# A hybrid encoder on one core: TensorE's order of state-space units and attention steps written out, matrices prepared in three parts and three units ahead

## The chip, the core and the metric

One core of a Trainium2 chip runs the whole kernel. Its engines are TensorE (PE; its weight loads are listed as PEld), VectorE (DVE), ScalarE (ACT), GpSimd (POOL) and SyncE (SP). Each works through its own queue in order; semaphores tie the queues together. The metric is the device time of one execution in microseconds, from start to end.

## The reference

Two layers of an encoder over 512 positions of width 1024, float32. The first layer joins a state-space mixer and grouped-query attention; the second is a recurrent block. Each is followed by a feed-forward part. The change lies in the first layer's mixer alone, so only that is shown.

```python
# state-space mixer, per direction (0 forward, 1 backward)
bu_re = jnp.einsum("bsgc,gpc->bsgp", uf, bb_re)
bu_im = jnp.einsum("bsgc,gpc->bsgp", uf, bb_im)
_, _, h_re, h_im = lax.associative_scan(_complex_linear_combine,
    (abar_re, abar_im, bu_re, bu_im), reverse=(direction == 1), axis=1)
y = y + (jnp.einsum("bsgp,gcp->bsgc", h_re, c_re[direction])
         - jnp.einsum("bsgp,gcp->bsgc", h_im, c_im[direction]))
...
g = jax.nn.gelu(y)
out = g * jax.nn.sigmoid(g @ glu_w + glu_b)
# attention, per block of 128 queries
s = jnp.einsum("bqkgd,bskd->bkgqs", q_blk, kf)
p = jax.nn.softmax(s, axis=-1)
o = jnp.einsum("bkgqs,bskd->bqkgd", p, vf)
# both are joined
mix = jnp.concatenate([y_s5, y_att], axis=-1) @ hyb_w_out[e]
```

## The kernel before

The mixer runs as eight **units**, four groups of columns (`pg`) times two directions (`d`), while attention runs as 32 **steps**, one for a head and a block of 128 queries. Steps and units share the engines; they do not depend on each other. What is left of attention behind the eight units is done in the **fill**, together with the gate's and the output's first products.

A unit has these parts, by the names in the code:

- `s5_prep` builds its matrices: complex products on GpSimd (L341, L343, L345), copies on ScalarE (L356 into `s5c`, L364 into `s5bt`, L369 into `s5bx`), four transposes on TensorE (L363). `s5_lag` follows: sixteen small products on TensorE (L406) and four sums on VectorE into `s5dc` (L415 for d = 0, L421 for d = 1).
- `s5_phase` copies phase tables on ScalarE (L384 to L390).
- `s5_states` has two halves. Each is a product on TensorE (L441, into PSUM `pb` in the first half and `p` in the second), three operations on VectorE that turn it by the phase (L446, L447, L448) and two scans (L455).
- `s5_turn` turns the states back: four products on GpSimd (L466, L468, L467, L469 in the order of its queue), two sums on VectorE (L472 needs L466 and L468, L473 needs L467 and L469), and sixteen matmuls on TensorE (L477) that add the unit's output to `py`.
- After two units, `s5_out` adds the direct part (L488), copies (L490) and transposes (L493, L494); `s5_ut` brings the next group's input (L500, L502).

A step of attention has scores (L967, L968), their maximum on VectorE (L970, out `esum`), the exponential on ScalarE (L972), four transposes (L980) with a copy (L982), and for two steps together sixteen products with the values (L989). The transposes are those of an earlier step, so a step doesn't wait for its own exponential.

PSUM has two banks `p5` for all that the code calls `p` (the second half's states, L363, L406, L493, L500 and the small L686), one `pb`, one `py`, two for scores, one each for `po` and `pt`.

The loop calls units in turn, with `STEPS[i]` steps of attention in each, and calls `prep(i + 2)` in unit i; units 0 and 1 are prepared ahead of it. In units 3 and 4 it also closes a pair of adaptive vectors (L686, L691). The order of calls is not the order on the engines: a scheduler in the framework orders each engine's queue, TensorE's too, by its own estimate of when things are ready. Behind the loop, TensorE's order is the written one.

## Time and profile before

| what | value |
|---|---|
| median of 3 runs | 1255.64 us (1254.99 to 1257.53) |
| the profiled execution | 1256.23 us |
| its span, first to last instruction | 1254.4 us |
| mean granted clock of TensorE | 0.959 |
| busy: TensorE | 1161.8 us (93%) |
| busy: VectorE | 804.5 us (64%) |
| busy: ScalarE | 532.3 us (42%) |
| busy: GpSimd | 240.4 us (19%) |

Times inside the kernel are microseconds from the span's start. The loop of eight units and its steps lies between about 122 and 262 us, the fill between 265 and 305 us. Shares over the whole span say little on the loop, since its stretches have different limits: it is read from windows and from timelines of single engines. A granted clock of 1.00 is TensorE's upper level, 0.50 the lower. Rows that follow each other on VectorE overlap by about 0.08 us: an operation of 512 columns is listed with 0.68 us and the next one starts 0.60 later.

### The profile page before, as it was taken

What the parts mean: (1) busy time and instruction counts of PE and PEld (TensorE: products, weight loads), DVE (VectorE), ACT (ScalarE), POOL (GpSimd) and SP (SyncE); (2) the same over time, 40 slices, a digit from 0 to 9 for tenths busy, and PEclk for the clock granted to TensorE, in tenths of its full rate; (3) what the DMA queues carried; (4) which work ended last, traced back from release to release, by engine and by line L of the source; (5) the groups of instructions that cost most, each with busy time, mean ns of one, the idle gap of its engine ahead of it and who ended that gap; (6) DMA issues with size and microseconds to landing.
All of it is one profiled execution on the core that took longest, in us unless ns stands there. A gap on an engine that the chain in (4) does not pass through costs nothing.

```text
span 1254.4 us, 16894 instructions
## 1 busy us (share of the span) xinstructions
PE 1161.8 (93%) x6456; PEld 983.0 (78%) x6456; DVE 804.5 (64%) x1182; ACT 532.3 (42%) x962; POOL 240.4 (19%) x346
## 2 busy tenths in 40 slices
PE   3678798889999999999999999789999999999997
PEld 2568577667998888888888988569988888888887
DVE  7548897988789875678433789995753332445243
ACT  3147577645452332134322449853543321334130
POOL 9996995410000000000000053000000000000000
PEclk9989697979999999999999999789999999999998
DMA  9411301065538765667332332112242223322311
GB/s 337 130 56 58 113 20 35 2 201 153 194 108 272 265 205 190 208 204 248 102 101 85 101 109 76 51 56 79 73 129 88 98 101 101 90 96 101 101 34 67
DMA packets 83856, 151.74 MB, mean 121 GB/s; under 512 B 5696, under 2 KB 30272, under 8 KB 83776
## 3 DMA queue, kind: packets, MB, share of 16 engines
q1 hardware_dynamic: 75712, 137.04, 33.6%
q10 hardware_dynamic: 8064, 13.64, 3.5%
q8 instruction: 50, 0.82, 0.3%
q14 instruction: 30, 0.25, 0.1%
HBM read 148.55 MB, written 2.10 MB: 120 GB/s over the span
## 4 chain that ended last, share of the span: by engine, by line
PE 71%; DVE 13%; POOL 8%; ACT 3%; issue 2%; DMA 1%; SPq 0%; ACTq 0%; DVEq 0%; POOLq 0%
PE ps L560 13%; PE ps L561 12%; PE ps L559 12%; PE px L559 8%; PE px L561 8%; PE px L560 8%; DVE wl L513 2%; POOL tiny L76 1%; DVE actb L455 1%; DMA wr<-wout 1%; PE py L477 1%; PE po L989 1%; DVE ti L1411 1%; DVE hs L1410 1%; DVE esum L970 1%
## 5 line engine op out<-in xcount | busy, mean ns | idle before, releaser
L513 DVE TENSOR_TENSOR wl<-wr,wh 128x1024 fp32r<-128x1024 f32 (+2 forms) x175 | 211.3, 1208 | 298.4 <-ACT wh L512 291.5
L512 ACT CAST wh<-wr 128x1024 fp32r<-128x1024 f32 (+2 forms) x170 | 173.6, 1022 | 436.5 <-PE ps L560 200.1
L560 PE MATMUL ps<-actb,wh 128*128 128x512 f32 (+1 forms) x512 | 181.3, 354 | 0.1
L559 PE MATMUL ps<-acta,wh 128*128 128x512 f32 (+1 forms) x328 | 116.8, 357 | 0.0
L561 PE MATMUL ps<-acta,wl 128*128 128x512 f32 (+1 forms) x328 | 116.1, 355 | 0.0
L559 PE MATMUL ps<-hid,wh 128*128 128x512 f32 x288 | 112.1, 389 | 0.0
L561 PE MATMUL ps<-hid,wl 128*128 128x512 f32 x288 | 112.0, 389 | 0.0
L560 PE MATMUL ps<-hid,wh 128*128 128x512 f32 x288 | 112.0, 389 | 0.0
L560 PEld LDWEIGHTS ps<-actb,wh 128*128 128x128 f32 x512 | 97.7, 191 | 13.5 <-DVE actb L849 0.3
L559 PE MATMUL px<-hid,wh 128*128 128x512 f32 (+1 forms) x288 | 98.9, 343 | 0.0
L560 PE MATMUL px<-hid,wh 128*128 128x512 f32 (+1 forms) x288 | 98.5, 342 | 0.0
L561 PE MATMUL px<-hid,wl 128*128 128x512 f32 (+1 forms) x288 | 98.5, 342 | 0.0
L560 PE MATMUL px<-actb,wh 128*128 128x512 f32 (+1 forms) x224 | 85.5, 382 | 0.0
L641 DVE SCALAR_TENSOR_TENSOR acc<-wr,cact,acc 128x1024 f32<-128x1024 f32 x49 | 62.8, 1282 | 16.8 <-DMA wr<-ada_w 16.3
L559 PEld LDWEIGHTS ps<-acta,wh 128*128 128x128 f32 x328 | 63.0, 192 | 8.5
L561 PEld LDWEIGHTS ps<-acta,wl 128*128 128x128 f32 x328 | 62.7, 191 | 8.5
L1338 POOL MEMSET xp<- 128x2 f32 x8 | 0.7, 98 | 348.0 <-PE px L561 343.7
L559 PE MATMUL ps<-actc,wh 128*128 128x512 f32 (+1 forms) x184 | 65.1, 354 | 0.0
L561 PE MATMUL ps<-actc,wl 128*128 128x512 f32 (+1 forms) x184 | 64.8, 352 | 0.0
L559 PEld LDWEIGHTS ps<-hid,wh 128*128 128x128 f32 x288 | 54.1, 188 | 11.2
L560 PEld LDWEIGHTS ps<-hid,wh 128*128 128x128 f32 x288 | 54.1, 188 | 11.2
L561 PEld LDWEIGHTS ps<-hid,wl 128*128 128x128 f32 x288 | 54.0, 188 | 11.2
(504 smaller groups left out, 2709.8 us busy)
## 6 DMA issues: line engine op xcount, KB each, us to landing
wr<-w SPq DMA_DIRECT2D x128, 512.0 KB, 3.7
wr<-ada_w SPq DMA_DIRECT2D x56, 512.0 KB, 4.4
wr<-wout SPq DMA_DIRECT2D x16, 512.0 KB, 3.6
araw<-ada_w ACTq DMA_DIRECT2D x32, 256.0 KB, 3.1
wr<-win SPq DMA_DIRECT2D x16, 512.0 KB, 3.8
acta<-ada_w SPq DMA_DIRECT2D x16, 256.0 KB, 5.5
actb<-ada_w SPq DMA_DIRECT2D x16, 256.0 KB, 5.5
nt<-ada_w ACTq DMA_DIRECT2D x16, 256.0 KB, 2.9
```

Of the source, the lines that this page charges most:

```text
L76: self.eng.tensor_scalar(t, a, s, None, op0=op0)
L455: self.scan = V.tensor_tensor_scan(*z, 0.0, op0=ALU.mult, op1=ALU.add)
L477: mm(p4[:, x], h[:, o:o + P], c[:, x], start=(d == 0 and x == 0 and i == 0), stop=False, skip_group_check=True)
L512: nc.scalar.copy(hi, src)
L513: (lo_eng or nc.vector).tensor_tensor(lo, src, hi.bitcast(F32), op=ALU.subtract)
L559: mm(out, wh, xh, start=first and a == a0 and lead(o), stop=False, skip_group_check=True)
L560: mm(out, wh, xl, start=False, stop=False, skip_group_check=True)
L561: mm(out, wl, xh, start=False, stop=last and a == a0 + kk - 1, skip_group_check=True)
L641: nc.vector.scalar_tensor_tensor(acc, raw, self.ca[:, k:k + 1], acc, op0=ALU.mult, op1=ALU.add)
L970: nc.vector.reduce_max(nb, s, axis=AX.X, negate=True)
L989: self.nc.tensor.matmul(po[h2 * 64:h2 * 64 + 64, t * 128:(t + 1) * 128], self.vp[:, kb, p // 2], pts[h2][:, kb * 128:(kb + 1) * 128], star ...
L1410: V.tensor_tensor_scan(hs, a[:, 0], ti[:, 0], 0.0, op0=ALU.mult, op1=ALU.add)
```

## The change

`s5_prep` becomes a generator of three parts (products and copies; transposes; the lag), `s5_states` yields after each half, `s5_out` has two parts, and `s5_turn` hands back a function that issues L477 later. The loop is written out as `unit(i)`: the whole of it stands in `manual()`, in which TensorE keeps the order of the code. The other engines' queues are still ordered by the scheduler. Unit 2 is prepared ahead of the loop and unit i+3 in unit i, one unit earlier than before. Of the attention steps, 25 are taken in the loop (2 in unit 0, 3 in each of the seven others, 2 behind them), where it was 23. The number of instructions of each engine is otherwise the same, and the program behind the loop is the same apart from the two steps. Lines of the new kernel are 4 to 10 higher (L441 is L445, L472 and L473 are L475 and L476, L477 is L483, L970 is L980, L686 is L696).

```diff
-STEPS = ((2, 2),) * 5 + ((2, 1),) + ((0, 0),) * 2
+STEPS = ((0, 0, 2),) + ((1, 1, 1),) * 7
+LAST = 2
...
+        sl0 = 3 if d == 0 else 0
+        bx = []
+        for j, src in enumerate((vr, vi)):
+            t = self.tl(tp, f"s5bx{j}", [P, 4, 4, 16], bufs=1)
+            A.copy(t, src[:, :, sl0].unsqueeze(2).to_broadcast([P, 4, 4, 16]))
+            bx.append(t)
+        yield
...
         self.s5u[(pg, d)] = bt, cs
-        return bx, cs
+        yield
+        self.s5_lag(tp, pg, (bx, cs), d)
+        yield
...
                 self.scan = V.tensor_tensor_scan(*z, 0.0, op0=ALU.mult, op1=ALU.add)
-        return vr, vi
...
+            yield vr, vi
...
+        def outputs(py):
+            p4 = py.rearrange("p (x g n) -> p x g n", x=4, g=2)
+            for i, (h, c) in enumerate(((a, cr), (vr, ci))):
+                for x in range(4):
+                    o = (x % 2 * 2 + x // 2) * P
+                    mm(p4[:, x], h[:, o:o + P], c[:, x], start=(d == 0 and x == 0 and i == 0), stop=False, skip_group_check=True)
+
+        return outputs
...
-        for i in range(8):
...
+        def steps(n):
+            for _ in range(n):
+                self.step(att)
+
+        def outputs(i):
+            if i % 2 == 0:
+                pys.append(self.psum("py"))
+            turns[i](pys[i // 2])
+
+        def unit(i):
             pg, d = i // 2, i % 2
+            pr = prep(i + 3) if i < 5 else iter(())
+            next(pr, None)
             if d == 0:
                 gts.append(self.tl(self.hp, "h", [P, 512], bufs=9))
             e = self.s5_phase(lp, pg, d, self.POST[i][0])
             if i == 3:
                 self.s5_tables(sp, 1)
+            st = self.s5_states(lp, pg, d, *e, uts[pg])
+            next(st)
+            steps(STEPS[i][0])
+            v = next(st)
+            next(st, None)
+            turns.append(self.s5_turn(pg, d, e[0], *v, self.POST[i][1]))
+            steps(STEPS[i][1])
+            so = iter(())
+            if i:
+                outputs(i - 1)
+                if d == 0:
+                    so = out(pg - 1)
+                    next(so)
+            next(pr, None)
+            if d == 0 and pg < 3:
+                uts.append(self.s5_ut(lp, sz[pg + 1]))
+            steps(STEPS[i][2])
+            next(so, None)
+            next(pr, None)
+            if i == 4:
+                next(pr, None)
+                pctx.close()
+                self.weights(rctx, 3, 2, side="right")
             if i in FIN:
...
+        turns = []
+        with self.manual():
+            for _ in prep(2):
+                pass
+            uts.append(self.s5_ut(lp, sz[0]))
+            for i in range(8):
+                unit(i)
+            steps(LAST)
+            outputs(7)
+            for _ in out(3):
+                pass
```

What this moves is seen at three places. In the names, `pb_` and `p_` are the states of a unit's two halves, `pa_` scores, `actb` states and their turned sums; the numbers tell buffers apart.

TensorE, around the end of unit 3 (its second half is `p_446` before and `p_447` now; `pb_486` and `pb_490` are unit 4's first half). Before:

```order
L477 MATMUL py_1833<-s5c_109,actb_1799 128x128 x4
L441 MATMUL pb_486_2233<-s5ut_2021,s5bt_1911 64x128 x8
L980 MATMUL pt_1967<-consts_sb,pexp_1855 128x128 x4
L686 MATMUL p_472_2177<-ones,h_810 128x1 x4
L956 MATMUL pt_1974<-consts_sb,qr_1129 128x128
```

Now:

```order
L1049 MATMUL pt_2126<-consts_sb,tmp_2124 128x128 x4
L990 MATMUL pt_2139<-consts_sb,pexp_2039 128x128 x4
L410 MATMUL p_471_2146<-s5c_104,s5bx_433_1993 64x128 x2
L410 MATMUL p_471_2146<-s5c_105,s5bx_434_1995 64x128 x2
L410 MATMUL p_471_2146<-s5c_104,s5bx_433_1993 64x128 x2
L410 MATMUL p_471_2146<-s5c_105,s5bx_434_1995 64x128 x2
L696 MATMUL p_473_2161<-ones,h_810 128x1 x4
L445 MATMUL pb_490_2213<-s5ut_1925,s5bt_1744 64x128 x8
```

The small L686 (L696 now) stood behind unit 4's first state product and two other products; now it stands between the lag of unit 6 and that state product. It takes the PSUM bank of unit 3's second half in both.

TensorE, where unit 1's output is added. Before, from its first half on (`pb_444` is unit 3's):

```order
L477 MATMUL py_1457<-s5c_104,actb_1653 128x128 x4
L967 MATMUL pa_376_1767<-kth_1102,q_305_1487 128x512
L968 MATMUL pa_376_1767<-ktl_1103,q_305_1487 128x512
L406 MATMUL p_413_1922<-s5c_116,s5bx_411_1918 64x128 x2
L406 MATMUL p_413_1922<-s5c_117,s5bx_412_1920 64x128 x2
L406 MATMUL p_413_1922<-s5c_116,s5bx_411_1918 64x128 x2
L406 MATMUL p_413_1922<-s5c_117,s5bx_412_1920 64x128 x2
L980 MATMUL pt_1773<-consts_sb,pexp_1687 128x128 x4
L989 MATMUL po_1566<-pts_1765,vp 64x128
L441 MATMUL pb_444_2046<-s5ut_1607,s5bt_1730 64x128 x8
L477 MATMUL py_1457<-s5c_105,actb_1619 128x128 x4
```

Now (`p_405` is unit 2's second half):

```order
L445 MATMUL p_405_1860<-s5ut_1562,s5bt_1437 64x128 x8
L977 MATMUL pa_409_1884<-kth_1102,q_332_1569 128x512
L978 MATMUL pa_409_1884<-ktl_1103,q_332_1569 128x512
L990 MATMUL pt_1890<-consts_sb,pexp_1755 128x128 x4
L483 MATMUL py_1735<-s5c_104,actb_1698 128x128 x4
L483 MATMUL py_1735<-s5c_105,actb_1643 128x128 x4
L496 MATMUL py_1735<-s5cd_1383,s5ut_1464 128x2x64 x4
L371 MATMUL p_415_1914<-consts_sb,s5vr_1781 128x128 x2
L371 MATMUL p_415_1914<-consts_sb,s5vi_1782 128x128 x2
L510 MATMUL p_416_1920<-consts_sb,h_814 128x128 x4
```

The two halves of L477 stood apart, with unit 3's first state product between them; now they stand together (L483) behind unit 2's second state product.

VectorE, from unit 4's first half (before) and from unit 4's end (now), up to unit 5's first half (`pb_544` before, `pb_522` now). Before:

```order
L455 SCALAR_TENSOR_TENSOR actb_2229<-s5m4t_2220,pb_486_2233 128x255
L455 SCALAR_TENSOR_TENSOR actb_2230<-s5m4t_2220,pb_486_2233 128x255
L472 TENSOR_TENSOR actb_2076<-actb_2076,actb_2077 128x511
L446 TENSOR_TENSOR s5m_2257<-s5e_2219,p_488_2248 128x512
L447 TENSOR_TENSOR p_488_2248<-s5e_2219,p_488_2248 128x512
L448 TENSOR_TENSOR p_488_2248<-p_488_2248,s5m_2257 128x512
L473 TENSOR_TENSOR actb_2042<-actb_2042,actb_2043 128x511
L455 SCALAR_TENSOR_TENSOR actb_2229<-s5m4t_2220,p_488_2248 128x255
L455 SCALAR_TENSOR_TENSOR actb_2230<-s5m4t_2220,p_488_2248 128x255
L446 TENSOR_TENSOR s5m_2482<-s5e_2459,pb_544_2473 128x512
```

Now:

```order
L459 SCALAR_TENSOR_TENSOR actb_2209<-s5m4t_2200,p_498_2256 128x255
L459 SCALAR_TENSOR_TENSOR actb_2210<-s5m4t_2200,p_498_2256 128x255
L980 TENSOR_REDUCE esum_1198<-pa_511_2323 128x1
L475 TENSOR_TENSOR actb_2271<-actb_2271,actb_2272 128x511
L476 TENSOR_TENSOR actb_2209<-actb_2209,actb_2210 128x511
L425 SCALAR_TENSOR_TENSOR s5dc_120<-p_516_2350,consts_sb,s5dc_120 128x4x16
L425 SCALAR_TENSOR_TENSOR s5dc_120<-p_516_2350,consts_sb,s5dc_120 128x4x32
L701 TENSOR_TENSOR mod_2166<-p_517_2367,cols_sb 128x4
L425 SCALAR_TENSOR_TENSOR s5dc_120<-p_516_2350,consts_sb,s5dc_120 128x4x48
L425 SCALAR_TENSOR_TENSOR s5dc_120<-p_516_2350,consts_sb,s5dc_120 128x256
L450 TENSOR_TENSOR s5m_2396<-s5e_2373,pb_522_2387 128x512
```

Before, the sums L472 and L473 of one unit stand within the halves of the next one: between those here are three operations on states, and two scans follow. Now L475 and L476 of unit 4 stand right behind its last scan and one maximum, ahead of unit 5's first operation (L450 on `pb_522`).

## Rows read from the trace of the kernel before

**Rows 1.** Windows: stretch, length, each engine's busy time, PEclk (granted clock), DMA.

```profile
134.00:163.30 29.30, 24.34 (x132) 17.59 (x131) 27.01 (x42) 15.96 (x35) 27.20 (x39) 0.64 0.37 110
163.30:193.00 29.70, 25.39 (x256) 19.90 (x253) 29.63 (x50) 24.38 (x54) 29.52 (x41) 1.00 0.00 1
193.00:210.00 17.00, 15.74 (x88) 12.88 (x89) 14.80 (x27) 12.16 (x27) 12.36 (x21) 0.50 0.20 63
210.00:221.00 11.00, 11.00 (x104) 9.40 (x104) 4.21 (x9) 7.61 (x19) 0.00 (x0) 1.00 0.01 1
221.00:246.20 25.20, 23.24 (x225) 18.04 (x222) 24.43 (x43) 15.88 (x34) 10.47 (x17) 1.00 0.00 1
...
265.00:305.00 40.00, 39.33 (x243) 29.46 (x244) 35.65 (x54) 19.98 (x40) 0.98 (x1) 0.92 0.54 174
...
334.00:1254.40 920.40, 895.97 (x4593) 764.14 (x4591) 545.26 (x755) 353.77 (x521) 34.71 (x44) 0.98 0.38 122
```

**Rows 2.** Timeline, TensorE: start, length, operation, idle time before it and its releaser.

```profile
170.65 1.09 PE L406 MATMUL p<-s5c,s5bx 128*64 128x128 f32 x16
...
174.18 1.16 PE L477 MATMUL py<-s5c,actb 128*128 128x128 f32 x8 [0.47 <-DVE actb L473]
...
194.26 1.86 PE L686 MATMUL p<-ones,h 128*128 128x1 f32 x8 [2.08 <-DVE actb L455]
...
204.48 2.07 PE L477 MATMUL py<-s5c,actb 128*128 128x128 f32 x8
...
244.32 1.16 PE L477 MATMUL py<-s5c,actb 128*128 128x128 f32 x8 [0.80 <-DVE actb L473]
```

**Rows 3.** Waits of VectorE, 163.3 to 246.2 us: total, times, longest.

```profile
DVE esum L970 <- PE pa L968: 7.0, 4, 3.8
DVE s5m L446 <- POOL actb L466: 0.7, 1, 0.7
DVE acta L513 <- ACT acta L512: 0.7, 1, 0.7
```

**Rows 4.** Timeline, VectorE, behind unit 4's states.

```profile
204.04 1.25 DVE L455 TENSOR_TENSOR_SCAN actb<-s5m4t,p 128x255 f32<-128x255 f32 x2
...
208.10 0.68 DVE L472 TENSOR_TENSOR actb<-actb,actb 128x511 f32<-128x511 f32 x1
208.70 1.25 DVE L455 TENSOR_TENSOR_SCAN actb<-s5m4t,pb 128x255 f32<-128x255 f32 x2
```

**Rows 5.** Timeline, GpSimd, unit 4's turn.

```profile
205.91 1.09 POOL L468 TENSOR_TENSOR actb<-s5e,actb 128x511 f32<-128x511 f32 x1
...
208.15 1.57 POOL L469 TENSOR_TENSOR actb<-s5e,actb 128x511 f32<-128x511 f32 x1
```

**Rows 6.** Timeline, VectorE and ScalarE, at the loop's start.

```profile
133.94 0.68 DVE L446 TENSOR_TENSOR s5m<-s5e,pb 128x512 f32<-128x512 f32 x1
...
155.72 0.58 ACT L364 COPY s5bt<-p 128x512 f32<-128x512 f32 x1 [6.06 <-DVE h L673]
```

**Rows 7.** Timeline, VectorE and TensorE, behind the last scan.

```profile
254.79 0.72 DVE L472 TENSOR_TENSOR actb<-actb,actb 128x511 f32<-128x511 f32 x1
...
255.56 2.08 PE L477 MATMUL py<-s5c,actb 128*128 128x128 f32 x8 [2.49 <-DVE actb L472]
```

**Rows 8.** Timeline, TensorE, one step of attention in the fill.

```profile
283.29 1.09 PE L989 MATMUL po<-pts,vp 128*64 128x128 f32 x16
284.31 0.50 PE L967 MATMUL pa<-kth,q 128*128 128x512 f32 x1
...
284.88 0.60 PE L980 MATMUL pt<-consts_sb,pexp 128*128 128x128 f32 x4
285.23 0.48 PE L559 MATMUL pb<-actb,wh 128*128 128x512 f32 x1
```

**Rows 9.** VectorE's group of L472, 163.3 to 246.2 us, and one timeline row.

```profile
L472 DVE TENSOR_TENSOR actb<-actb,actb 128x511 f32<-128x511 f32 x6 | 5.3, 883 | 0.0
...
228.40 1.52 DVE L472 TENSOR_TENSOR actb<-actb,actb 128x511 f32<-128x511 f32 x1
```

More of the change, by code (lines that the diff above doesn't have):

```diff
@@ L364, in s5_prep @@
         A.copy(bt.rearrange("p i x m -> p (i x m)"), ps)
-        sl0 = 3 if d == 0 else 0
-        bx = []
-        for j, src in enumerate((vr, vi)):
-            t = self.tl(tp, f"s5bx{j}", [P, 4, 4, 16], bufs=1)
-            A.copy(t, src[:, :, sl0].unsqueeze(2).to_broadcast([P, 4, 4, 16]))
-            bx.append(t)
         self.s5u[(pg, d)] = bt, cs
-        return bx, cs
+        yield
+        self.s5_lag(tp, pg, (bx, cs), d)
+        yield
     def s5_phase(self, sp, pg, d, eng):
@@ L455, in s5_states, with s5_turn @@
                 self.scan = V.tensor_tensor_scan(*z, 0.0, op0=ALU.mult, op1=ALU.add)
-        return vr, vi
-    def s5_turn(self, pg, d, e, vr, vi, eng, py):
+            yield vr, vi
+    def s5_turn(self, pg, d, e, vr, vi, eng):
         mm = self.nc.tensor.matmul
@@ L469, in s5_turn @@
         eng.tensor_tensor(vi[:, dst], er, vi[:, dst], op=ALU.mult)
-        p4 = py.rearrange("p (x g n) -> p x g n", x=4, g=2)
         V = self.nc.vector
@@ L473, in s5_turn @@
         V.tensor_tensor(vr[:, dst], vr[:, dst], vi[:, dst], op=ALU.add)
-        for i, (h, c) in enumerate(((a, cr), (vr, ci))):
-            for x in range(4):
-                o = (x % 2 * 2 + x // 2) * P
-                mm(p4[:, x], h[:, o:o + P], c[:, x], start=(d == 0 and x == 0 and i == 0), stop=False, skip_group_check=True)
+        def outputs(py):
[5 more added lines that the diff above has]
+        return outputs
     def s5_out(self, sp, pg, ut, py, gt):
@@ L490, in s5_out @@
         nc.scalar.copy(g, py.rearrange("p (x t c) -> p t x c", x=8, t=4))
+        yield
         ps = self.psum("p5")
@@ L493, in s5_out @@
             nc.tensor.transpose(ps[:, t * 128:(t + 1) * 128], g[:, t].rearrange("p g c -> p (g c)"), self.ident)
-        return nc.scalar.copy(gt, ps)
+        nc.scalar.copy(gt, ps)
+        yield
     def s5_ut(self, sp, sz):
@@ L1124, in hybrid @@
         self.banks(pbctx, ps=6)
-        prep = lambda i: self.s5_lag(tp, i // 2, self.s5_prep(tp, i // 2, i % 2, bc, self.PREP[i]), i % 2)
+        prep = lambda i: self.s5_prep(tp, i // 2, i % 2, bc, self.PREP[i])
         x = []
@@ L1165, in hybrid @@
         self.s5_in(win, u, 0, sz)
-        prep(0)
-        prep(1)
+        for i in range(2):
+            for _ in prep(i):
+                pass
         self.attn_kv(hp, psk)
@@ L1188, in hybrid @@
         out = lambda pg: self.s5_out(lp, pg, uts[pg], pys[pg], gts[pg])
-        for i in range(8):
+        def steps(n):
[6 more added lines that the diff above has]
+        def unit(i):
             pg, d = i // 2, i % 2
-            if i == 0:
-                uts.append(self.s5_ut(lp, sz[0]))
-            if d == 1 and pg < 3:
-                uts.append(self.s5_ut(lp, sz[pg + 1]))
+            pr = prep(i + 3) if i < 5 else iter(())
+            next(pr, None)
             if d == 0:
@@ L1199, in hybrid @@
                 self.s5_tables(sp, 1)
-            v = self.s5_states(lp, pg, d, *e, uts[pg])
-            if d == 0:
-                pys.append(self.psum("py"))
-            self.s5_turn(pg, d, e[0], *v, self.POST[i][1], pys[pg])
-            for _ in range(STEPS[i][0]):
-                self.step(att)
-            if i + UNITS - 3 < 8:
-                prep(i + UNITS - 3)
-                if i + UNITS - 3 == 7:
-                    pctx.close()
-                    self.weights(rctx, 3, 2, side="right")
+            st = self.s5_states(lp, pg, d, *e, uts[pg])
[21 more added lines that the diff above has]
+                self.weights(rctx, 3, 2, side="right")
             if i in FIN:
                 fins.pop(0)()
-            for _ in range(STEPS[i][1]):
-                self.step(att)
-            if d == 0 and pg > 0:
-                out(pg - 1)
-        out(3)
+        turns = []
[8 more added lines that the diff above has]
+            for _ in out(3):
+                pass
         for f in fins:
```

## The prediction

> **What bounds the kernel now.** I read the windows of the span first. From 334 us to the end (920 of 1254 us) TensorE is busy 97% at a granted clock of 0.98, and the change leaves that part alone [rows 1]. Between 134 and 334 us the stretches differ. From 163 to 193 us VectorE is busy 29.63 of 29.70 us and GpSimd 29.52; from 193 to 210 us the clock is 0.50; from 210 to 221 us VectorE works 4.21 of 11.0 us while TensorE is full; from 221 to 246 us VectorE is full again (24.43 of 25.2); from 265 to 305 us, the fill, TensorE is full (39.33 of 40.0) [rows 1]. So the loop of eight units is VectorE's, but for one hole, and the fill is TensorE's.
>
> The timeline of TensorE tells the hole's history. At 194.26 us a small product (L686) has stood for 2.08 us behind a scan whose PSUM bank it takes; the clock of the stretch behind is 0.50 (1.2 GHz), and eight matmuls of L477 take 2.07 us there, where they take 1.16 at full clock [rows 1, 2]. TensorE falls behind its queue, and VectorE waits for scores: 7.0 us in four waits, the longest 3.8 [rows 3]. That is most of what VectorE waits for in units 2 to 7, from unit 1's last scan (ends 163.3) to unit 7's (ends 246.2): 9.3 us in five lines, of which rows 3 has the three largest (7.0, 0.7, 0.7) and the other two are 0.6 and 0.3, for the state products [rows 3].
>
> **The change, part by part.** The sum is made against the profiled execution (1256.23 us), which lies 0.59 us above the median of the runs shown; I take that off at the end.
>
> (a) *The written order of TensorE.* No instruction is added or dropped on TensorE. Per unit it now does the first state product, a step of attention, the second, a step, the output product of the unit before (L477), the transposes of unit i+3, a third step, and that unit's lag product. L477 stands whole behind the second state product of the next unit, where its input is half a unit old. Its waits for the turn (0.47 us at 174.18, 0.80 at 244.32) go [rows 2]; worth nothing directly, since VectorE was busy beside them. L686 still stands behind a scan, but now with two steps (1.44 us each, by (f)), two L477 (2.1), four transposes of L363 (0.7), those of L956 and L1039 (0.9) and L406 (1.09 [rows 2]) between the state product and it: 7.7 us of TensorE's work, against 5.4 us of VectorE's over the same stretch (five operations at 0.60 and two pairs of scans at 1.17). The 0.9 and 0.7 are estimates, at 0.11 to 0.18 for a matmul of 128 columns, as L477's 1.16 for eight gives with its overlap. So the 2.08 us wait should go, with it the slow stretch and the 7.0 us. That is the gain: **-9.3 us**, with the short waits; ends -9.3 and 0 (the hole stays).
>
> (b) *VectorE's order.* This is the price. Before, the sums that close a turn (L472, L473) stood inside the next unit's work. Now, for units 1, 3, 4 and 6, both stand ahead of the next unit's first L446, and there they wait for GpSimd. By unit 4's rows: its second pair of scans starts at 204.04 and ends 1.17 later, at T = 205.21; L468 runs from 205.91 to 207.00, so L472 can start at T+1.8; L469 starts at 208.15 and takes 1.57, undisturbed 1.09 as L468 does, so L473 can start at T+4.1 to 4.5 [rows 4, 5]. What the new order puts ahead of each sum (0.60 for an L970, L446, L513 or L1042, as 208.10 to 208.70 for L472 [rows 4]; I take 0.65 for L472, and 0.45 for L1034 and L1036 together):
> unit 1: nothing, then L472 and one L970: 1.8 + 1.05 = 2.85; unit 2: 1.05 of work ahead, enough behind: 0.75; unit 3: one L970, later L1042: 1.2 + 1.05 = 2.25; unit 4: one L970, then nothing: 1.2 + 1.65 = 2.85; unit 5: L1036, L970 and one L446: 0.25; unit 6: L513, later one L970: 1.2 + 1.05 = 2.25.
> Sum **+11.2 us**. Ends: 5.6, if half falls beside a late state product of TensorE, and 13, if L469 takes 1.57 in the four units that wait for it.
>
> (c) *VectorE's work.* In units 2 to 7 it has one L970 more (18 for 17: +0.6) and one lag set less, since unit 2's is done before the loop (four operations, -1.2): **-0.6 us**.
>
> (d) *The start.* Unit 0's first L446 starts at 133.94 us [rows 6], behind the adaptive weights' transfers, which set it now and still will; unit 2's lag (1.2 us of L415) moves ahead of it, out of unit 0. Attention begins later: ScalarE's copy of unit 2's transposes waits 6.06 us at 155.72, queued behind a DMA whose buffer VectorE releases [rows 6], and that copy now stands ahead of the first steps. I take **+1 us** for unit 1's last scan; ends -2.3 (all of VectorE's idle time in 134 to 163.3, 29.30 less 27.01 [rows 1]) and +3 (half of the copy's wait).
>
> So the last scan moves by -9.3 + 11.2 - 0.6 + 1 = +2.3 us. For waits that TensorE's order makes within a unit I add **+1** (in 163 to 193 VectorE has 0.07 of any [rows 1]): +3.3.
>
> (e) *The tail.* Behind the last scan VectorE's rows are the same up to L472 at 254.79 [rows 7]. TensorE waited 2.49 us there and ran L477 at half clock (2.08) [rows 7]. Now it has two more steps to do meanwhile, and their transposes stand ahead of L477 where before one stood between L488 and L493. The rest of the chain can start up to 2 us sooner: **-1 us**; ends 0 (order and clock as before) and -4 (those 2, and full clock for two L477, 2 x 0.92).
>
> (f) *The fill.* Two of its twelve steps are gone. One step takes TensorE 0.57 for the scores (284.31 to 284.88), 0.35 for four transposes (to 285.23), and half of 1.02 for sixteen L989 (283.29 to 284.31): 1.43 us [rows 8]. TensorE is the fill's bound: **-2.9 us**. The next weights' transfers are issued behind the last step and follow it.
>
> Sum: +3.3 - 1 - 2.9 = **-0.6 us**; 1256.23 - 0.6 - 0.59 = **1255.0 us**.
>
> **The rivals.** *Even trade* (above): -4 to +4 us, by the middle parts of its ends. For it: both large terms are of like size in one trace. Against: each hangs on who arrives first.
>
> *Clean gain:* TensorE's first product of the next unit comes as late as the turn's sum, so half of (b) costs nothing (-5.6), and the tail keeps full clock (-2): -8.2 us, 1247.4. For it: TensorE was busy 23.24 of 25.20 us in 221 to 246, nearly a bound itself. Against: VectorE was the fuller there, 24.43 [rows 1].
>
> *Slower by the clock:* the waits of (b) hold back scores, since an L970 stands behind a waiting L472. TensorE then runs dry at the turn, as at 192 to 194 us, and the clock falls again. The price is the hole that I counted as gone: +7.0 us for one [rows 3], so +6.4 and 1262; 1269 for two. It decides when TensorE's gap at a turn reaches the 2.08 us ahead of the slow stretch; gaps of 0.47 and 0.80 did not bring it [rows 2].
>
> *Slower by the turn itself:* L472 now follows L468 at once and so runs beside L467. At 228.40 it took 1.52 us where that at 208.10 took 0.68; the mean of six is 0.88 [rows 4, 9]. Six at 0.5 to 0.64 more: +3 to +4, 1258 to 1259. The Trainium skill states it too ("GPSIMD Engine Reference", section 8, Key points): GpSimd shares its SBUF interfaces with VectorE, and contends with VectorE instructions that have two SBUF inputs, as L472 has. By that rule every turn would pay, here +4; the trace agrees at 228.40, but at 208.10 the other engine's L469 was the long one.
>
> *The order does nothing:* the same engines bound the same stretches: 1255 to 1256.5.
>
> **How the numbers follow.** Even trade 0.44; clean gain 0.26; the clock 0.16; the turn 0.10; nothing 0.04. A measurement of this kernel can tell about 0.2%, 2.5 us, from no change. Faster: 0.26 and 0.13 of the even trade's lower part, 0.39. Slower: 0.16, 0.08 of the turn and 0.11 of the even trade's upper part, 0.35. Same: the rest, 0.26. The time is that of the even trade. The range leaves out 0.1 at each end: the lower part of the clean gain, below 1246, and the dearer part of the clock, above 1265.
>
> **What would show it.** Right: no stretch of clock 0.50 between 190 and 210 us, and no L970 that waits over 1 us for L968 in units 4 and 5; waits of L472 or L473 for GpSimd in six turns, about 11 us in sum; the last scan at 246 to 252 us; ten steps in the fill, some 3 us shorter. Wrong: waits of L446 for TensorE in their place (the clean gain, if the last scan ends before 244), two or more stretches of half clock between 165 and 245 us (the clock), or an L472 of over 1.2 us on average (the turn).

## The result and the profile after

The changed kernel takes 1276.06 us (median of 4 runs, 1272.32 to 1278.98), the kernel before 1256.14 (1254.99 to 1257.53): a ratio of 1.0156, 95% interval 1.0126 to 1.0187. It is slower by some 20 us; the forecast was 1255.0 and the range ended at 1265.

| what | before | after |
|---|---|---|
| the profiled execution | 1256.23 us | 1274.96 us |
| its span | 1254.4 us | 1272.8 us |
| mean granted clock | 0.959 | 0.959 |
| busy: TensorE | 1161.8 us | 1154.3 us |
| busy: VectorE | 804.5 us | 809.7 us |
| unit 1's last scan ends | 163.3 | 166.2 |
| unit 7's last scan ends | 246.2 | 262.5 |
| the fill begins (first L559, now L569) | 264.87 | 284.39 |
| the fill's last sum (L1042, now L1052) starts | 306.00 | 321.08 |

The first reading is TensorE's idle time, span less busy: 92.6 us before, 118.5 now, 25.9 more. Its busy time is 7.5 less, so the span is 18.4 longer. The windows of after show where; those of before with the same meaning are [rows 1].

```profile
134.00:150.00 16.00, 4.11 (x15) 3.00 (x16) 13.93 (x18) 7.00 (x13) 15.86 (x25) 0.50 0.50 155
150.00:166.20 16.20, 13.52 (x82) 9.71 (x84) 14.64 (x23) 9.26 (x23) 11.73 (x16) 0.54 0.17 50
166.20:185.90 19.70, 14.89 (x144) 12.52 (x141) 15.85 (x25) 13.34 (x30) 19.70 (x26) 0.99 0.00 1
185.90:203.30 17.40, 14.28 (x113) 10.97 (x112) 12.23 (x22) 12.83 (x27) 10.48 (x17) 0.72 0.18 61
...
247.30:262.50 15.20, 13.10 (x122) 10.44 (x122) 10.72 (x18) 5.56 (x13) 5.27 (x8) 1.00 0.00 2
262.50:284.40 21.90, 11.12 (x69) 8.75 (x67) 17.27 (x21) 9.70 (x20) 9.03 (x7) 0.77 0.38 124
...
352.00:1272.00 920.00, 894.83 (x4574) 762.93 (x4573) 544.63 (x752) 352.83 (x519) 35.06 (x44) 0.98 0.38 122
```

From 352 us on TensorE is as full as it was. Between 134 and 150 us it is busy 4.11 of 16.0 us, at a clock of 0.50, and in the units behind it has gaps: 14.89 of 19.70, 14.28 of 17.40. VectorE, which was full from 163 to 193 us [rows 1], now works 15.85 of 19.70 and 12.23 of 17.40 us. In 262.5 to 284.4, the tail, TensorE works 11.12 of 21.90.

VectorE's waits between the last scans of units 1 and 7 (166.2 to 262.5 us), which answer [rows 3], are 19.5 us in sum, where they were 9.3:

```profile
DVE rsum L1044 <- ACT pexp L982: 4.8, 1, 4.8
DVE esum L980 <- PE pa L978: 4.2, 4, 2.1
DVE actb L476 <- POOL actb L473: 2.4, 2, 1.4
DVE actb L475 <- POOL actb L472: 2.0, 1, 2.0
DVE s5m L450 <- PE pb L445: 2.0, 1, 2.0
DVE actb L476 <- POOL actb L469: 1.0, 1, 1.0
DVE actb L475 <- POOL actb L436: 1.0, 1, 1.0
```

The four lines with POOL as releaser are 6.4 us: waits for GpSimd's turn. Scores (L980) are 4.2 instead of 7.0. New is one wait of 4.8 us for an exponential.

*The start.* TensorE's timeline, at the place where unit 3's transposes (L371) and the next group's input (L510) stand ahead of the first attention steps:

```profile
133.07 0.63 PE L371 MATMUL p<-consts_sb,s5vi 128*128 128x128 f32 x2
139.75 1.12 PE L510 MATMUL p<-consts_sb,h 128*128 128x128 f32 x4 [6.05 <-ACT s5bt L372]
140.66 1.06 PE L966 MATMUL pt<-consts_sb,qr 128*128 128x128 f32 x4
...
144.57 0.78 PE L977 MATMUL pa<-kth,q 128*128 128x512 f32 x1
```

L510 takes a PSUM bank from which ScalarE has to copy first (L372), and stands 6.05 us at the head of the queue. The query transposes (L966) and the first scores (L977) stand behind it; they start at 140.66 and 144.57. ScalarE's timeline shows why the copy is late:

```profile
135.40 0.93 ACT L357 COPY s5c<-s5cv 64x320 f32<-64x320 f32 x2 [1.24 <-POOL s5cv L346]
...
138.16 0.93 ACT L357 COPY s5c<-s5cv 64x320 f32<-64x320 f32 x2 [1.83 <-DVE h L683]
139.11 0.59 ACT L372 COPY s5bt<-p 128x512 f32<-128x512 f32 x1
```

The transposes that L372 copies are done at 133.70. Ahead of it stand two pairs of copies: the first waits 1.24 us for GpSimd, the second 1.83 us behind the start of a transfer whose buffer VectorE releases (L683).

*Units 2 and 3.* ScalarE's timeline, then TensorE's and VectorE's at the same time:

```profile
181.01 1.87 ACT L357 COPY s5c<-s5cv 64x320 f32<-64x320 f32 x4 [2.62 <-POOL s5cv L346]
182.91 0.69 ACT L982 ACTIVATE pexp<-pa,esum 128x512 f32<-128x512 f32 x1
...
184.06 0.60 ACT L372 COPY s5bt<-p 128x512 f32<-128x512 f32 x1
184.67 1.28 ACT L306 ACT_TABLE_LOAD   x1
...
189.55 1.28 ACT L982 ACT_TABLE_LOAD   x1
190.85 0.69 ACT L982 ACTIVATE pexp<-pa,esum 128x512 f32<-128x512 f32 x1
```

```profile
180.51 0.38 PE L371 MATMUL p<-consts_sb,s5vi 128*128 128x128 f32 x2
184.71 0.66 PE L510 MATMUL p<-consts_sb,h 128*128 128x128 f32 x4 [3.82 <-ACT s5bt L372]
185.12 0.56 PE L977 MATMUL pa<-kth,q 128*128 128x512 f32 x1
...
191.66 0.20 DVE L1044 RECIPROCAL rsum<-esum 128x8 f32<-128x8 f32 x1 [4.83 <-ACT pexp L982]
```

GpSimd is late with a matrix, and ScalarE waits 2.62 us at its copies (L357, four of them, 1.87 in all). Behind them stand an exponential and the copy L372 that frees the bank for TensorE's L510. TensorE waits 3.82 us at L510, with scores behind it. When these are done, ScalarE is at other work: between 184.67 and 190.85 it loads the activation table twice (1.28 us each) and makes phase tables (L306). So the exponential runs at 190.85 only, and VectorE waits 4.83 us for it. A late matrix and ScalarE's own queue have gone through to TensorE and VectorE.

*The tail.* TensorE, then VectorE:

```profile
271.53 0.79 PE L977 MATMUL pa<-kth,q 128*128 128x512 f32 x1 [8.33 <-ACT pexp L982]
...
277.80 1.95 PE L483 MATMUL py<-s5c,actb 128*128 128x128 f32 x16
...
262.49 3.17 DVE L1064 SCALAR_TENSOR_TENSOR nt<-nt,h 128x512 f32<-128x512 f32 x2
265.58 4.48 DVE L523 TENSOR_TENSOR wl<-wr,wh 128x1024 fp32r<-128x1024 f32 x2
269.99 0.68 DVE L980 TENSOR_REDUCE esum<-pa 128x1 f32<-128x512 f32 x1
...
271.19 0.68 DVE L475 TENSOR_TENSOR actb<-actb,actb 128x511 f32<-128x511 f32 x1
```

The next step's scores need a PSUM bank that an exponential has to read first; that exponential needs a maximum (L980), which stands in VectorE's queue behind 7.5 us of work for the layer's next part (L1064, L523). TensorE waits 8.33 us, where it waited 2.49 before [rows 7]. The last output product (L483) stands behind two steps that come after this wait. Its input L475 starts 8.6 us behind the last scan in both kernels (254.79 before [rows 7], 271.19 now), but L483 starts 6.6 us behind L475, where L477 started 0.8 behind L472 [rows 7].

*The turn.* VectorE's group of L475 (L472 before, 883 ns [rows 9]), three of its rows, and GpSimd's L471 at the same moments:

```profile
L475 DVE TENSOR_TENSOR actb<-actb,actb 128x511 f32<-128x511 f32 x6 | 7.6, 1260 | 3.0 <-POOL actb L472 2.0 <-POOL actb L436 1.0
...
222.30 1.57 DVE L475 TENSOR_TENSOR actb<-actb,actb 128x511 f32<-128x511 f32 x1
...
237.67 1.77 DVE L475 TENSOR_TENSOR actb<-actb,actb 128x511 f32<-128x511 f32 x1
...
249.54 0.69 DVE L475 TENSOR_TENSOR actb<-actb,actb 128x511 f32<-128x511 f32 x1 [0.98 <-POOL actb L436]
...
222.24 1.09 POOL L471 TENSOR_TENSOR actb<-s5e,actb 128x511 f32<-128x511 f32 x1
...
237.61 1.28 POOL L471 TENSOR_TENSOR actb<-s5e,actb 128x511 f32<-128x511 f32 x1
...
249.58 1.60 POOL L471 TENSOR_TENSOR actb<-s5e,actb 128x511 f32<-128x511 f32 x1
```

The mean is 1260 ns. Where L475 took 1.57 or 1.77, GpSimd's product beside it took 1.09 or 1.28; where it took 0.69, GpSimd's took 1.60.

### The profile page after: what moved, and what is told of

Its sections match the earlier page's. It is cut to its first block, busy times and chain, and to the rows that moved or that the text cites. A ratio compares the mean times of both kernels' runs of the same rounds, so it can differ in the third digit from the quotient of the medians.

```text
span 1272.8 us, 16901 instructions
## 1 busy us (share of the span) xinstructions
PE 1154.3 (91%) x6456; PEld 977.8 (77%) x6456; DVE 809.7 (64%) x1182; ACT 533.2 (42%) x962; POOL 241.0 (19%) x346
## 4 chain that ended last, share of the span: by engine, by line
PE 70%; DVE 13%; POOL 9%; ACT 4%; issue 2%; DMA 2%; ACTq 0%; DVEq 0%; POOLq 0%
PE ps L570 12%; PE ps L569 12%; PE ps L571 12%; PE px L569 8%; PE px L570 8%; PE px L571 8%; DVE wl L523 2%; POOL tiny L77 1%; DMA nt<-ada_w 1%; DVE actb L459 1%; DMA araw<-ada_w 1%; DVE h L683 1%; DVE esum L980 1%; POOL s5ptmp L344 1%; DVE ti L1449 1%
## 5 line engine op out<-in xcount | busy, mean ns | idle before, releaser
L523 DVE TENSOR_TENSOR wl<-wr,wh 128x1024 fp32r<-128x1024 f32 (+2 forms) x175 | 211.3, 1208 | 293.3 <-ACT wh L522 286.8
L569 PE MATMUL ps<-acta,wh 128*128 128x512 f32 (+1 forms) x328 | 117.2, 358 | 0.0
L569 PE MATMUL ps<-hid,wh 128*128 128x512 f32 x288 | 112.1, 389 | 0.0
L569 PE MATMUL px<-hid,wh 128*128 128x512 f32 (+1 forms) x288 | 98.9, 343 | 0.0
L651 DVE SCALAR_TENSOR_TENSOR acc<-wr,cact,acc 128x1024 f32<-128x1024 f32 x49 | 62.8, 1282 | 18.5 <-DMA wr<-ada_w 18.2
L569 PEld LDWEIGHTS ps<-acta,wh 128*128 128x128 f32 x328 | 63.5, 194 | 8.5
L569 PE MATMUL ps<-actc,wh 128*128 128x512 f32 (+1 forms) x184 | 65.1, 354 | 0.0
L569 PEld LDWEIGHTS ps<-hid,wh 128*128 128x128 f32 x288 | 54.1, 188 | 11.3
L571 PEld LDWEIGHTS ps<-hid,wl 128*128 128x128 f32 x288 | 54.1, 188 | 11.2
L570 PEld LDWEIGHTS ps<-hid,wh 128*128 128x128 f32 x288 | 54.1, 188 | 11.2
```

Of the source, the lines that this page charges most:

```text
L523: (lo_eng or nc.vector).tensor_tensor(lo, src, hi.bitcast(F32), op=ALU.subtract)
L569: mm(out, wh, xh, start=first and a == a0 and lead(o), stop=False, skip_group_check=True)
L570: mm(out, wh, xl, start=False, stop=False, skip_group_check=True)
L571: mm(out, wl, xh, start=False, stop=last and a == a0 + kk - 1, skip_group_check=True)
L651: nc.vector.scalar_tensor_tensor(acc, raw, self.ca[:, k:k + 1], acc, op0=ALU.mult, op1=ALU.add)
```

## The experiments

Times are medians of 4 or more runs, except one that is marked; ratios are to the kernel before on the same chip, with a 95% interval. The first runs ask which part of the change costs the time, the second which place in TensorE's order, the third what is left of the gain.

### Which part

**sched**: everything as in the changed kernel, TensorE's order left to the scheduler.

```diff
-        with self.manual():
+        with ExitStack():
```

> The changed kernel's code (three parts, three units ahead, L483 one unit later, 25 steps), with TensorE's order left to the scheduler again. Theory 'written order' (TensorE stands at the head of its written queue for ScalarE's copies, 11.2 us at L510 and 7.2 us at L977, and every unit's VectorE work then runs one after the other): back to within 4 us of the kernel before, 1252 to 1260 us, last scan at 244 to 250 us. Theory 'three ahead' (GpSimd and ScalarE do the matrices of unit i+3 too early, in front of turns and exponentials): stays at 1268 us or more.

Measured: 1249.45 us, ratio 0.9939 (0.9924 to 0.9954). That is below even the range of the theory 'written order'. So the written order costs 27 us (1.0156 less 0.9939, of 1256), and the rest of the change gains 7. By the marks of the table above, the profiled executions (spans of 1272.8 and 1247.9 us) lie 6.6 us apart at unit 1's last scan; 14.1 more come in units 2 to 7, 3.4 in the tail, 2.0 in the fill, and 1.3 are given back behind it. Of the 14.1, 12.4 are waits of VectorE: between unit 1's last scan and unit 7's (159.6 to 241.8 us here) they are 7.1 us instead of 19.5:

```profile
DVE s5m L450 <- PE p L445: 3.0, 1, 3.0
DVE s5m L450 <- PE pb L445: 2.0, 1, 2.0
DVE actb L475 <- POOL actb L472: 1.2, 1, 1.2
DVE esum L980 <- PE pa L978: 0.9, 1, 0.9
```

TensorE's timeline at the start shows what the scheduler does at the place above. The first four score matmuls are through before L510, which waits for the same copy:

```profile
136.03 0.55 PE L977 MATMUL pa<-kth,q 128*128 128x512 f32 x1
136.42 0.39 PE L978 MATMUL pa<-ktl,q 128*128 128x512 f32 x1
136.65 0.40 PE L977 MATMUL pa<-kth,q 128*128 128x512 f32 x1
136.88 0.40 PE L978 MATMUL pa<-ktl,q 128*128 128x512 f32 x1
139.65 1.12 PE L510 MATMUL p<-consts_sb,h 128*128 128x128 f32 x4 [2.38 <-ACT s5bt L372]
```

One line of code was changed, but not only TensorE's order with it: the scheduler orders the other queues to suit, and VectorE's waits for GpSimd, 6.4 us with the written order, are 1.2 here. The 27 us belong to the written order with all that follows from it; no run separates TensorE's queue from VectorE's.

**sched_steps**: scheduler's order and the old 23 steps, `STEPS = ((0, 2, 2),) * 5 + ((0, 2, 1),) + ((0, 0, 0),) * 2`, `LAST = 0`. **sched_ahead2**: scheduler's order with matrices two units ahead (`prep(i + 2)` in unit i, no `prep(2)` before the loop).

> TensorE's order left to the scheduler, three units ahead, but the steps as before the change: four in each of units 0 to 4, three in unit 5, none in 6 and 7, 23 in all. Theory 'three ahead gains': within 2 us of 1249.5, or 2 to 3 us more for the two steps in the fill. Theory 'steps gain': 1254 to 1258 us.

> TensorE's order left to the scheduler, and the matrices two units ahead instead of three; the rest as in the changed kernel. It tells what the 7 us under the kernel before come from. Theory 'three ahead gains' (VectorE was full from 140 to 190 us because the matrices were there): 1254 to 1258 us. Theory 'steps and deferral gain': within 2 us of 1249.5.

Measured: 1257.94 us, 1.001 (0.9999 to 1.002), and 1251.15, 0.9954 (0.9935 to 0.9974). With the old row of 23 steps the rest of the change is worth nothing; the gain of 7 us hangs on the steps. Whether on their number or their spread, these runs don't separate: the 25 are three to a unit, the 23 were four in each of the first five units. The third unit ahead would be worth 0.0015 of 1256, 1.9 us, but the intervals overlap.

**b_25**: the kernel before with 25 steps in the loop and nothing else of the change.

```diff
-STEPS = ((2, 2),) * 5 + ((2, 1),) + ((0, 0),) * 2
+STEPS = ((2, 0),) + ((2, 1),) * 6 + ((2, 3),)
```

> The kernel before with the steps alone changed: 25 in the loop, two in unit 0, three in units 1 to 6, five in unit 7, instead of 23 in units 0 to 5; two units ahead, the output product in its own unit, TensorE's order the scheduler's. If steps alone carry the gain of 7 us that the changed kernel has without the written order: 1248 to 1251 us. If it needs the three parts as well: 1254 to 1258 us.

Measured: 1250.65 us, 0.9957 (0.9940 to 0.9974). One line of the diff brings what the whole change brings under the scheduler, as far as these runs can tell them apart.

### Which place in the written order

**ut_first**: the next group's input (`s5_ut`, L510) ahead of the transposes L371, in the units and before the loop. **ahead2**: the written order, matrices two ahead. **pb_early**: the next unit's first state product ahead of a unit's third step. **pb_early_ut**: both ut_first and pb_early.

> The changed kernel with one edit: the input transposes of the next group (L510) stand ahead of the matrices' transposes (L371) in TensorE's written order, in the loop and ahead of it, so that they take a PSUM bank that waits for nothing of ScalarE. Theory 'written order, at this place': the three waits of L510 (11.2 us) go, unit 1 ends at 163 to 164 us (166.2 now), VectorE's wait of 4.83 us at 191.66 shrinks below 1.5; 1266 to 1270 us. Theory 'three ahead': the wait moves to the next product that needs the copy or the matrices; within 2 us of 1276. Theory 'turn' (the sums L475 and L476 wait for GpSimd ahead of the next unit): within 3 us of 1276.

> The changed kernel with matrices two units ahead, as before the change: unit 2 is prepared in unit 0, unit i+2 in unit i; TensorE's order still written out. Theory 'three ahead': ScalarE's copies L357 no longer wait for buffers that L483 holds (3.4 us) nor stand in front of exponentials, the first scores come 8 us earlier; 1260 to 1266 us. Theory 'written order': the same waits come at other places, 1272 to 1280 us.

> The changed kernel, written order kept, with one product moved: the first state product of unit i+1 (L445 into pb) stands behind the output product L483 of unit i-1, ahead of the third step, of that step's waits and of the lag, instead of behind them. VectorE then has the next unit's first half at hand while GpSimd turns unit i. Theory 'units one after the other' (what the written order costs is that VectorE runs dry between two units): VectorE's waits for GpSimd's sums and for pb fall from 8.4 us to below 3, the last scan comes 6 to 10 us earlier; 1264 to 1270 us. Theory 'steps' (what costs is that TensorE stands at the head of its queue for attention's exponentials and copies, 13 us and more): within 4 us of 1276.

> Both edits to the written order together: the next unit's first state product early, and the input transposes L510 ahead of the matrices' transposes. Theory 'units one after the other' and 'written order at L510' add up: 1261 to 1267 us. If TensorE only waits elsewhere, as much as the first edit alone, within 2 us.

Measured: 1273.01 us, 1.0125 (1.0107 to 1.0143); 1271.21, 1.0113 (1.0098 to 1.0128); 1274.16, 1.0135 (1.0114 to 1.0156); and 1277.95, 1.0175 (1.0155 to 1.0195). By the medians each change of one place brings 2 to 5 us of 27, but each interval overlaps the changed kernel's (1.0126 to 1.0187), and two of them together bring nothing; ahead2 lies between its two ranges, pb_early_ut above both of its own.

The traces show what becomes of a mended place. In ut_first all the signs of its theory came: TensorE's waits at L510 fall from 11.2 us to 2.9, unit 1's last scan ends at 162.9, VectorE's wait of 4.83 us is 0.3. But all of TensorE's waits from 122 to 262 us are 37.0 us, where they were 37.1: those of scores for an exponential (L977) have grown from 7.2 to 10.9. In ahead2 unit 3's last scan ends at 194.2, 9 us earlier than in the changed kernel. In both, unit 7's ends within 0.6 us of where it did: units 4 to 7 give back what was won.

**no_defer**: a unit's output product L483 in its own unit (`outputs(i)`), not in the next.

> The changed kernel with the output product L483 in its own unit, behind the second step, instead of one unit later. It now waits for the unit's own turn on GpSimd (sums ready 4 us behind the last scan), and holds the third step, the transposes and the next state product behind it. Theory 'written order': every wait at the head of TensorE's queue counts, so 8 units x 2 to 4 us, 1285 to 1300 us. Theory 'turn' (VectorE is the bound and waits for GpSimd in any case): within 4 us of 1276, since VectorE waits for the same sums already.

Measured: 1332.97 us, 1.0609 (1.0591 to 1.0626), 57 us more than the changed kernel and far above both ranges. The deferral is what this written order lives by; without it TensorE stands at each turn (its largest waits, 122 to 320 us: total, times, longest):

```profile
PE py L483 <- DVE actb L475: 43.2, 7, 19.2
```

**steps_behind**: `STEPS = ((0, 0, 2),) + ((0, 0, 3),) * 7`. **steps_none**: all 25 steps behind the loop (`((0, 0, 0),) * 8`, `LAST = 25`).

> The changed kernel, written order kept, with the three steps of a unit together behind its two state products, the output product and the transposes, instead of one between each. Theory 'steps': the second state product no longer stands behind a step, VectorE works both halves in one go while TensorE does the steps; but the next unit's products stand behind three; 1266 to 1272 us. Theory 'units one after the other': more of each unit is in a row, 1276 to 1284 us.

> The changed kernel, written order kept, with no step of attention inside the units: all 25 stand behind unit 7. The time as a whole says little (the steps then run alone); read the loop. Theory 'steps' (TensorE stands at the head of its queue for attention's round trip over VectorE and ScalarE, and the state products behind it come late): from unit 1's last scan to unit 7's at most 70 us (96.3 in the changed kernel, 18 maxima less are 10.8 of it), VectorE's idle time there below 8 us (19.5). Theory 'matrices' (the products wait for ScalarE's and GpSimd's preparation): over 85 us, L510 and L410 still wait for ScalarE.

Measured: 1302.25 us (1.0362) and 1319.34 (2 runs). steps_behind is above both of its ranges: with three steps in a block, TensorE's waits of scores for an exponential are 30.9 us in seven (122 to 300 us), the longest 12.2. In steps_none the loop from unit 1's last scan to unit 7's is 77.6 us, between what the two theories expected. VectorE, with no attention in its way, is still idle for 15.8 of them (20.5 of 96.3 in the changed kernel), 7.7 of these for the lag's products (L410):

```profile
DVE s5dc L419 <- PE p L410: 3.9, 2, 2.2
DVE s5dc L425 <- PE p L410: 3.8, 2, 2.2
```

So the units wait for TensorE and GpSimd without the steps as well, though less.

**written_0_3** and **written_4_7**: the written order only up to unit 3, or only from unit 4 to the end. The diff is that of written_0_3: the second loop stands outside `manual()`.

```diff
-            for i in range(8):
+            for i in range(4):
                 unit(i)
...
+        for i in range(4, 8):
+            unit(i)
...
```

> Only the preparation of the third group and units 0 to 3 keep the written order of TensorE; units 4 to 7, the last steps and the tail are left to the scheduler. Theory 'start' (the loss is made while the attention begins late: in the written kernel the last scan of unit 3 ends at 203.3 against 190.4 where the scheduler orders everything): the 12.9 us of the first half stay, 1262 us or more. Rival 'second half' (units 4 to 7 add 7.8 us by the scans, and the tail the rest of the 26.6): at most 1256 us.

> The other half: the scheduler orders everything up to unit 3, the written order stands for units 4 to 7, the last two steps and the last group's output. If the losses of the halves add up to the 26.6 us between the scheduler's order (1249.45) and the written one, this one takes 1249.5 plus what the run of units 0 to 3 leaves: 'start' 1262 us at most, 'second half' 1267 us or more. If both halves are well below half of the loss, it is made where the halves meet, by the order of the whole.

Measured: 1261.66 us, 1.0033 (1.0017 to 1.0050), and 1257.64, 1.0001 (0.9990 to 1.0011). Over the scheduler's 0.9939 the halves lose 11.8 and 7.8 us; both together lose 27.3. So each half holds a part, the first nearly half of the loss, and by the medians 7.7 us come only with the whole; with the four intervals taken together that is 3 to 13 us.

**first_steps**: unit 0's two steps ahead of unit 3's transposes and of L510 (`STEPS = ((0, 2, 0),) + ...`).

> The written order throughout, but unit 0's two steps of attention stand ahead of the transposes of unit 3 and of the second group's product, where they stood behind them. Theory 'start' (the first scores come at 144.57, about 10 us later than before, since TensorE waits up to 6.05 us for group 1's products ahead of them): 5 to 8 us go, 1268 to 1271 us. If the steps themselves are the brake, whatever their place (a step waits for ScalarE, a unit for the step): within 3 us of 1276.

Measured: 1274.06 us, 1.0141 (1.0109 to 1.0174): 2 us, within what was expected of the steps as the brake. The run tests the late start only in part: the first scores come at 140.72 instead of 144.57, not at 136.03 as in sched, since another instruction, a transpose of queries (L966), now waits 6.05 us for ScalarE. In ut_first they come at 137.17. In neither does unit 7's last scan end more than 0.6 us earlier. Attention's late start was the most visible hole in the trace, but mending it alone isn't worth the 27 us.

**late_parts**: in unit i the transposes and the lag of unit i+2, then the products of unit i+3, so that the former find their inputs done.

```diff
-            pr = prep(i + 3) if i < 5 else iter(())
-            next(pr, None)
+            pr = prs.pop()
...
             next(pr, None)
-            if i == 4:
-                next(pr, None)
+            next(pr, None)
+            prs.append(prep(i + 3) if i < 5 else iter(()))
+            next(prs[0], None)
+            if i == 5:
...
```

> The written order, but the transposes and the lag of a unit's matrices stand one unit later than their products and copies: unit i ends with the products of unit i+3 and has the transposes and the lag of unit i+2 in its middle, so that their inputs are half a unit old or more. Theory 'head of the queue' (TensorE stands behind matrices that GpSimd and ScalarE have not finished: its waits for s5bt are 11.2 us in three, the longest 6.05): these waits go to 3 us or less, and 8 to 15 us of the time with them, 1261 to 1268 us. If the waits go and others take their place, as in the three runs that moved one part: 1270 us or more.

Measured: 1273.29 us, 1.0126 (1.0104 to 1.0148). TensorE's waits, 122 to 262 us:

```profile
PE pa L977 <- ACT pexp L982: 6.5, 4, 3.2
...
PE pt L990 <- ACT q L968: 4.6, 4, 3.6
PE pt L966 <- ACT q L968: 3.4, 1, 3.4
PE p L510 <- ACT s5bt L372: 3.3, 2, 2.4
```

L510 waits 3.3 us where it waited 11.2 in the changed kernel, as that theory expected, but all of TensorE's waits in this stretch only fall from 37.1 to 31.1 us: those of L966 and L990 for the queries' copies (`q`) grow from 5.0 to 8.0. Unit 3's last scan ends 9 us earlier, unit 7's within 0.5 us of where it did. The time falls by 3.7 us (1.0156 less 1.0126, with intervals that overlap), not by 8 to 15. Late matrices are at most a small part of the loss.

### What is left of the gain

**sched_27** and **sched_29**: scheduler's order, `LAST = 4` and `LAST = 6`. **b_27**: the kernel before with `((2, 0),) + ((2, 1),) * 6 + ((2, 5),)`.

> TensorE's order left to the scheduler, three units ahead, and two more steps in the loop (27 in all, 8 left for the fill). If what made 25 steps better than 23 by 8 us is work moved out of the fill, where a step costs 1.43 us of TensorE's time at least, into TensorE's free time in the loop, two more give 2 to 4 us again: 1245 to 1248 us. If it was the even spread over the units (three in each, none of four), they give nothing or cost: 1249 to 1253 us.

> The scheduler's order, three units ahead, with 29 of the steps in the loop instead of 25 or 27. 25 to 27 gave 2.7 us (1249.45 to 1246.75), or 1.35 us a step. If a step in the loop still lies beside work of VectorE and its relief behind the loop continues: 1244 to 1246 us. If the loop is full by now, so that a step more holds the units up by as much as it saves later: 1247 us or more.

> The kernel before with 27 steps of attention in the loop (2 in unit 0, 3 in units 1 to 6, 7 in unit 7), none of the change beside it. If the two steps that took the scheduled new kernel from 1249.45 to 1246.75 do the same here: 1247 to 1249 us, and the change's parts add 1 to 2 us. If the earlier preparation is what makes room for them: 1250 us or more.

Measured: 1246.75 us, 0.9921 (0.9897 to 0.9945); 1249.39, 0.9942 (0.9924 to 0.9959); 1247.95, 0.9933 (0.9907 to 0.9959). By the medians two steps more give 2.7 us in either kernel, and another two give them back; the intervals overlap. sched_27 is the fastest version, 29 us faster than the changed kernel, and b_27, the kernel before with another row of numbers, can't be told from it.

## Why the prediction was wrong, point by point

The sum was made of shifts of the last scan, the tail and the fill. All are from the profiled executions:

| step | predicted | measured |
|---|---|---|
| (a) VectorE's waits other than for GpSimd's turn, with the +1 for waits within a unit | -8.3 | +3.8 |
| (b) VectorE's waits for GpSimd's turn | +11.2 | +6.4 |
| (c) VectorE's work, and what else is left of the stretch | -0.6 | +3.2 |
| (d) start | +1 | +2.9 at unit 1 |
| last scan | +3.3 | +16.3 |
| (e) tail | -1 | +3.2 |
| (f) fill | -2.9 | -4.4 |
| behind the fill | 0 | +3.3 |

**(a)** is the step that failed: with its +1 it is 12 us off, and what was measured lies outside the ends that it gave itself (-9.3 and 0). The wait of L686 did go. But the maxima of units 4 and 5 still waited 3.3 us in two, where none over 1 us was the sign for it. I had let VectorE's other waits vanish and priced what a written order brings inside a unit at +1, since VectorE had waited 0.07 us between 163 and 193 us [rows 1]. That row tells what the scheduler's order does, which can put other work ahead of an instruction that will be late, as it did in sched at 136 us; it is no bound for a written one. The same code has 7.1 us of VectorE's waits with the scheduler's order and 19.5 with the written one. TensorE's queue is worked through in order, and I never listed, for each of its instructions in the new order, the engine it waits for. One row pointed there: ScalarE's copy at 155.72 [rows 6] was named, but only as an end of (d), for unit 1's last scan and at half of its 6.06 us. It is unit 3's copy, not unit 2's as the prediction has it: the fourth of its kind in ScalarE's timeline. The 6.06 us are ScalarE's idle time before it; what counted was that L510 and all of attention's first steps now stand behind this copy on TensorE. It is the copy for which L510 waits 6.05 us in the profile after, there behind copies that wait for GpSimd and for a transfer's start. The Trainium skill has the order of the queues as well ("PSUM — Partial Sum Buffer", Engine vs sequencer instructions): ScalarE's, VectorE's and GpSimd's queues are strictly first in, first out, and matmuls start and complete in program order. The trace agrees: nothing passed the waiting L510 in 6.05 us.

**(b)** had the right mechanism. By unit: 1 predicted 2.85, measured 3.04; 6 predicted 2.25, measured 2.41; 4 predicted 2.85, measured 0.98; 2, 3 and 5 predicted 0.75, 2.25 and 0.25, measured none. In units 2 and 3 VectorE had been waiting for something else: 4.83 us for an exponential and 2.07 for scores. So nearly half of the price went, as the clean gain had it, but into other waits.

**(c)** The +3.2 is what the other rows leave of the stretch; VectorE's busy time grew by 2.7 of it. That is mostly the rival of the turn: six L475 at 1260 instead of 883 ns are 2.3 us, below the 3 to 4 that it named. Its sign, an L472 of over 1.2 us on average, is there; it was not the cause of 20 us.

**(d)** came out at its bound of +3 for unit 1's scan. What the bound left out is that TensorE fell behind with attention, at the lower clock: 0.50 from 134 to 150 us and 0.54 from there to 166.2, where it was 0.64 from 134 to 163.3 [rows 1]. In sched it was 0.67 from 130 to 150 and 1.00 from there to 160. What share of the loss the clock has is not shown.

**(e)** took the wrong sign. Two more steps at the tail were to fill TensorE's wait. They come behind it instead: a step's maximum stands in VectorE's queue behind the next part's work, so TensorE waits 8.33 us, and then the two steps hold up L483 by 6.6 us after its input. Sched has the same two steps, but there L483 starts 0.8 us behind L475 (251.84 behind 251.07), and the tail is as long as before (18.5 us; 18.7 before).

**(f)** was right in kind: ten steps, and 4.4 us instead of 2.9. But 3.3 us come back behind the fill. They go with the steps and not with the written order: the stretch behind the fill's last sum is longer than before by 4.6 us in sched and by 2.6 in b_25, which also have two steps fewer in the fill. What makes it longer I have not traced.

Of the rivals, *slower by the clock* named a lower clock and a time of 1262 to 1269, but by VectorE's wait at the turn. The half clock came at the start, and TensorE ran dry by its own queue. Its sign, two or more slow stretches between 165 and 245 us, is there too (0.50 from 186 to 192 us, 0.70 from 197 to 202), but sched has 0.72 and 0.66 in the same stretches and is 25 us shorter, so these two are not what separates the orders. The *clean gain* fell with (a). What was missing is a rival for the written order itself: a chain of waits over TensorE, ScalarE and VectorE.

What is shown: the written order costs 27 us, and the same code under the scheduler's order is 7 us faster than before. That by the medians no place that was tried carries more than about 5 of them is shown by five runs (ut_first, ahead2, pb_early, first_steps, late_parts), and that they lie in both parts of the loop by the two halves. That it is TensorE's position at the head of its queue, whatever the instruction, is the reading that fits them, and it is argued: VectorE's changed queue may have its share. A written order that loses nothing was not tried, and whether there is one stays open.

## What to carry to other kernels

When an engine's order is written by hand, list for each instruction what it waits for and who stands behind it, and price every wait that the old order stepped around: here rows of the old order bounded none of them. A hole mended at one place is worth only what is still won at the end of the loop: in ahead2 and late_parts 9 us won by unit 3 were gone by unit 7. So test the order as a whole against the scheduler's with all else equal. And try the smallest line of a diff alone: here the row of steps brought all the gain that these runs can tell.

## What was not expected of the hardware

- VectorE's two-input sum and GpSimd's product, when they run together, share the cost unevenly: three pairs of rows show L475 at 1.57, 1.77 and 0.69 us with GpSimd's at 1.09, 1.28 and 1.60. The Trainium skill states that the two contend ("GPSIMD Engine Reference", section 8, Key points). The trace agrees, and shows which one is held: the one that starts second, by 0.06, 0.06 and 0.04 us in the three pairs. All 56 pairs of a closing sum and a product of the turn that start within 0.12 us of each other, over the profiles of all kernels here, go the same way: with VectorE first (42) its sum takes 0.68 to 0.69 us and the product 1.57 to 1.80; with GpSimd first (14) the product takes 1.09 to 1.28 and the sum 1.56 to 1.79.
